# Two seven-product groups per pair in place of three in the out projection, and a table of paces for the weight sums kept in DRAM

## The chip, the cores and the metric

The kernel runs on one core of one Trainium2 chip. The metric is the device time of one execution in microseconds; before the change the median of 3 runs is 2548.02 us (2546.67 to 2549.71).

## The reference

A two-layer decoder trunk on 256 tokens of width 2048, all in float32. What matters here is the first layer and the chain of matrix products:

```python
zxbcdt = h @ in_proj                       # 2048 -> 2 x 4096 + 2 x 1024 + 64
z, xbc, dt_raw = split(zxbcdt)
...                                        # conv, SiLU, chunked scan -> y
y = y.reshape(bsz, seq, D_INNER) * silu(z)
yg = y.reshape(bsz, seq, SSM_GROUPS, 512)  # 8 groups of 512
yg = yg * rsqrt(mean(yg * yg, axis=-1) + EPS)
h = h + (yg.reshape(...) * gnorm_w) @ out_proj   # 4096 -> 2048
h = h + (silu(hn @ wg) * (hn @ wu)) @ w_down     # 2048 -> 2 x 5632 -> 2048
...                                        # second layer: attention (q, k, v, o), then the same kind of FFN
```

## The kernel before, in words

Every float32 product is made of three TensorE products in the type fp32r. A weight piece of two k-tiles by 512 columns (128x1024 in SBUF, `wraw`, 512 KB) is split by ScalarE into a rounded part `whi` (line 272) and by VectorE into the rest `wlo` (line 278); the activations lie in SBUF as such a pair already (`xT`, a "slot" of four k-tiles). Then hi*hi, hi*lo and lo*hi are added up in PSUM (lines 554 to 556). A piece makes 12 matmuls of 512 columns: two k-tiles, two halves of the tokens, three products.

`stream` runs over all pieces of the program in order. SyncE (SP) loads the weights, in units of 512 KB, six of them ahead (`RAW`); the splits are four pieces ahead of TensorE (`SPL`). A unit is loaded when the oldest of the six `wraw` buffers has been split, so the load queue follows VectorE.

Two neighbouring blocks of 512 output columns form a pair (`pair`). For some of the k groups (`kg`, four k-tiles each), named in `crossed`, the pair's 2x2x2 block product is made with seven products in place of eight (`Group`, `cross_step`, the order of the seven is f, d, c, a, e, g, b; lines 466 to 469). That takes 42 matmuls in place of 48, and needs sums of activation blocks (`xS`, made by `sums_from`, or from a finished slot by `add_sums`) and sums of weight blocks. Two of the weight sums of each group are made in DRAM: `next_sum` issues on SP a copy of one weight block into a DRAM tile `wsum` (line 375), and on GpSimd's queue the adding of the other block to the sum that was copied before (line 377). `sums` is one list over the whole program, in the order of use: the out projection, the first FFN's up and down projections, the attention's out projection, the second FFN's.

When a sum is made is set in `stream`: at every n-th unit loaded, `PACE` calls `next_sum` once. `PACE = (24, 224, 6, 10)` starts at unit 24, with n = 6 up to unit 224 and n = 10 from there. When a unit that is a sum comes up for loading and the sum is not made, `load` calls `next_sum` until it is: the next copy is issued, the adding is issued, and the load waits on SP until the adding has landed. All later loads stand behind it.

The out projection (8 groups kg, two pairs) crosses the groups `WOUT = (2, 4, 6)`. In a pair the uncrossed groups are laid out as left-block pieces (L) first and right-block pieces (R) behind them, with all the R put ahead of the next crossed group, so the first pair runs L0 L1 R0 R1 G2 L3 R3 G4 L5 R5 G6 L7 R7. Ahead of it stand the eight z blocks; block g gives `z_done(g)` (SiLU) and then `gate_y(g)`: multiply (line 1061), square (1064), the root on GpSimd (573), scale (1069), eight transposes on TensorE (586) and the split into the slot `ys[g]`. Gates run one after the other. The L pieces of the pair use PSUM buffers that z block 6 frees, the R pieces those of block 7, whose SiLU waits for gate 5. When the first group of a pair comes to its second product, d, `finish_all(False)` puts everything of the gates that is still open ahead of it, since the group takes four PSUM banks.

Of the kernel before, what the change touches and what calls it, by code (L numbers as in the profile page):

```python
# [24 lines left out]
G = 8  # L25
# [8 lines left out]
BIG = 1e30  # L34
KT = 4

WOUT, DN0, DN1 = (2, 4, 6), (3, 7), (3, 5, 7, 9)

WARM = 9
RAW = 6  # L40
SPL = 4

PACE = (24, 224, 6, 10)


LAT = 0.4
# [185 lines left out]
def kernel(ctx: ExitStack, tc: tile.TileContext, xT_d, x_d, cols_d, rows_d, wdt_d, win_d,  # L232
# [17 lines left out]
    def nm(s):  # L250
        uid[0] += 1
        return f"{s}_{uid[0]}"
# [4 lines left out]
    def bank(shape):  # L257
        return mis.tile(shape, F32, tag="mis", name=nm("mis"))
# [109 lines left out]
    def next_sum():  # L368


        new = next((v for v in sums if v.tile is None), None)
        old = next((v for v in sums if v.tile is not None and not v.made), None)
        if new is not None:
            new.tile = dram.tile([P, 2, NB], F32, name=nm("wsum"))
            nc.sync.dma_start(out=new.tile, in_=new.one)
        if old is not None:
            nc.gpsimd.dma_start(out=old.tile, in_=old.other, accum_op=ALU.add)  # L377
            old.made = True
# [8 lines left out]
    def load(u, apart=False, before=None):  # L387
        u.raw = wraw.tile([P, len(u.ks), u.width], F32, tag="wraw", name=nm("wraw"))
        src = u.src
        if isinstance(src, Sum):  # L390
            while not src.made:
                next_sum()
            src = src.tile
        for js in u.pieces if apart else [range(len(u.ks))]:
            if before is not None:
                before([u.ks[j] for j in js])
            nc.sync.dma_start(out=u.raw[:, js[0]:js[-1] + 1, :], in_=src[:, js[0]:js[-1] + 1, :])
# [24 lines left out]
    def split_cross(group, name):  # L422

        us = group.units

        def add(out, in0, in1):
            flow.work("V", 1.22, flow.at["E"])
            nc.vector.tensor_tensor(out=us[out].raw, in0=us[in0].raw, in1=us[in1].raw, op=ALU.add)  # L428

        place, dead = {"e": "c", "b": "c"}, {"f": "f", "c": "d", "a": "a", "g": "g", "b": "c"}  # L430
        late = {"c": ("c", "c", "d"), "e": ("c", "c", "g")}
        src = us[place.get(name, name)].raw
        hi = wspl.tile([P, 2, NB], F32R, tag="whi", name=nm("whi"))
        lo = wspl.tile([P, 2, NB], F32R, tag="wlo", name=nm("wlo"))
        split(hi, lo, src)
        ready = flow.work("V", 1.22, flow.work("A", 1.05, flow.at["E"]) + LAT)
        if name in late:
            add(*late[name])
        if name in dead:
            us[dead[name]].dead = True  # L440
        return hi, lo, ready
# [40 lines left out]
    def stream(pre_load, pre_split):  # L482
        pieces, units = [], []
        for b in blocks:
            for u in b.units if isinstance(b, Block) else b:
                if isinstance(u, Group):
                    pieces += [(u, n) for n in Cross.ORDER]
                    units += u.units.values()
                else:
                    pieces += [(u, ks) for ks in u.pieces]  # L490
                    units.append(u)
        parts = {}
        loaded, dead = [0], [0]

        def load_on():
            while dead[0] < len(units) and units[dead[0]].dead:
                dead[0] += 1
            while loaded[0] < min(dead[0] + RAW, len(units)):
                i = loaded[0]
                if i in pre_load:  # L500
                    pre_load[i]()
                pace = PACE[2] if i < PACE[1] else PACE[3]
                if i >= PACE[0] and i % pace == pace - 1:
                    next_sum()
                load(units[i], i == 0, load_x0 if i < 2 else None)
                loaded[0] += 1

        def split_to(n):
            for i in range(len(parts), min(n, len(pieces))):
                u, js = pieces[i]  # L510
                if i in pre_split:
                    pre_split[i]()
                parts[i] = split_cross(u, js) if isinstance(u, Group) else split_piece(u, js)
                load_on()

        load_on()
        split_to(SPL - 1)
        held = deque()
        for i, (u, ks) in enumerate(pieces):
            split_to(i + SPL)  # L520
            if isinstance(u, Group):
                cross_step(u, ks, parts[i])
                continue
            b = u.blk
            nk = KT * len(b.xs)
            hi, lo, ready = parts[i]
            flow.work("E", 0.0, ready)
            if u.width < NB:
                if b.ps is None:
                    b.ps = bank([2 * u.width, T])  # L530
                for j, k in enumerate(u.ks[n] for n in ks):
                    both = hi[:, j].rearrange("p a n -> p (a n)")
                    s = slot_of(b.xs[k // KT])
                    nc.tensor.matmul(b.ps, lhsT=both, rhs=s[:, 0, k % KT, :], start=k == 0, stop=False)
                    nc.tensor.matmul(b.ps, lhsT=both, rhs=s[:, 1, k % KT, :], start=False, stop=k == nk - 1)
                flow.work("E", 0.22 * len(ks))
                if ks is u.pieces[-1]:
                    b.task = spawn(b.done(b.ps))
                continue
            if b.ps is None:  # L540
                held.append(b)
                if len(held) > 2:
                    flow.finish(held.popleft().task, evac=True)
                b.ps = [acc.tile([P, u.width], F32, tag="acc", name=nm("acc")) for _ in range(NT)]
            last = b.after is None and u is b.units[-1] and ks is u.pieces[-1]
            order = [(j, t) for j in range(len(ks)) for t in range(NT)]
            if last:
                order = [(j, t) for t in range(NT) for j in range(len(ks))]
            for n, (j, t) in enumerate(order):
                k = u.kg * KT + u.ks[ks[j]]  # L550
                s = slot_of(b.xs[k // KT])
                xh = s[:, 0, k % KT, t * P:(t + 1) * P]
                xl = s[:, 1, k % KT, t * P:(t + 1) * P]
                nc.tensor.matmul(b.ps[t], lhsT=xh, rhs=hi[:, j, :], start=u is b.units[0] and ks[j] == 0, stop=False)  # L554
                nc.tensor.matmul(b.ps[t], lhsT=xh, rhs=lo[:, j, :], start=False, stop=False)  # L555
                nc.tensor.matmul(b.ps[t], lhsT=xl, rhs=hi[:, j, :], start=False,  # L556
                                 stop=last and j == len(ks) - 1)
                if n % 2 == 1:
                    flow.work("E", STEP)
                    flow.pump()  # L560
            if last:
                finish_block(b)
        flow.finish_all()
# [59 lines left out]
    def add_sums(dst, apart=True):  # L623


        def run():
            if not dst.task.done:
                yield dst.task
            s = dst.tile
            for half in range(2):  # L630
                if apart:
                    y, x = (lambda c: (c[:, 0], c[:, 1]))(phase.tile([P, 2, NB], F32, tag="c4", name=nm("ysum")))
                else:
                    y, x = tok("y"), None
                y = y.rearrange("p (f t) -> p f t", t=T)
                part = [s[:, i, 2 * half:2 * half + 2, :].bitcast(F32) for i in range(2)]
                nc.vector.tensor_tensor(out=y, in0=part[0], in1=part[1], op=ALU.add)
                yield V(0.66)
                yield from sums_from(dst, half, y, x)
        dst.adder = spawn(run(), flow.lazy)  # L640
# [396 lines left out]
    ys = [Slot() for _ in range(G)]  # L1037

    def z_done(g):
        def run(ps):  # L1040
            if g >= 2:
                yield ys[g - 2].task
            zs = []
            for t in range(NT):
                z = tok("zs")
                nc.scalar.activation(z, ps[t], AF.Silu, scale=rstd[:, t:t + 1])  # L1046
                zs.append(z)
                yield A(0.57, SILU)
            ys[g].task = spawn(gate_y(g, zs), flow.mid)
            if g >= G - 2:  # L1050
                for kg in WOUT:
                    if (kg < G - 2) == (g == G - 2):
                        add_sums(ys[kg])
        return run

    def gate_y(g, zs):
# [325 lines left out]
```

## Time and profile before

| | |
|---|---|
| median of 3 runs | 2548.02 us (2546.67 to 2549.71) |
| the profiled execution | 2547.09 us; its span 2545.3 us, 1.8 us lie around the span |
| TensorE busy | 2497.1 us, 98%; granted clock 0.989 in the mean |
| VectorE, ScalarE, GpSimd busy | 1990.1, 1443.6 and 137.0 us |
| moved by DMA | 638.56 MB; 120 sums are copied and added |

A busy TensorE is not all of it: the granted clock has two levels, 1.2 and 2.4 GHz, and a clock of 0.5 of full speed stands for the lower one. So time is lost where TensorE is idle, and where it works at the lower level. The stages in order of time: z and scan up to about 521 us, out projection, first FFN up and down, attention from about 1400, second FFN up from about 1820, down from about 2300 to the end.

### The profile page before, as it was taken

The page shows a single profiled execution, that of the slowest core. Times are in us where ns is not written, and L with a number is a line of the kernel's source. Part 1 is how long each engine was busy: PE and PEld are TensorE (multiplying, and loading weights), DVE is VectorE, ACT ScalarE, POOL GpSimd, SP SyncE. Part 2 cuts the span into 40 slices and gives each one's busy share as a digit, 9 for nine tenths or more (in the row PEclk, how much of TensorE's full clock was granted, in tenths as well). Part 3 has the DMA queues.
Part 4 walks back from the last instruction along what each step waited for, and adds up shares of the span by engine and source line. Part 5 has one row for each costly group of instructions (what it writes and reads, how often), then busy time and mean ns, then how long its engine had stood idle before and what let it go on. Part 6 is the DMA issues. An engine that isn't in the chain of part 4 may idle for free.

```text
span 2545.3 us, 31879 instructions
## 1 busy us (share of the span) xinstructions
PE 2497.1 (98%) x11410; PEld 2064.3 (81%) x11410; DVE 1990.1 (78%) x2577; ACT 1443.6 (57%) x1815; POOL 137.0 (5%) x172
## 2 busy tenths in 40 slices
PE   9999999979999999999999999999999999999899
PEld 7888888868888888888888888888888877787787
DVE  6777777768788999998756667778889987788667
ACT  6566565555555665655544555566656654554444
POOL 0000000000000000000000011000000000000000
PEclk9999999989999999999999999999999999999899
DMA  7887777749988888887778777766778899987886
GB/s 265 252 254 240 224 234 240 237 144 307 278 256 252 290 259 282 258 290 238 256 228 268 221 210 226 205 193 219 237 260 280 270 296 270 293 293 233 264 281 230
DMA packets 174606, 638.56 MB, mean 251 GB/s; under 512 B 19408, under 2 KB 20064, under 8 KB 172912
## 3 DMA queue, kind: packets, MB, share of 16 engines
q1 hardware_dynamic: 155664, 563.05, 63.7%
q0 software_dynamic: 18784, 73.49, 15.8%
q8 instruction: 89, 1.46, 0.2%
q14 instruction: 69, 0.57, 0.1%
HBM read 634.28 MB, written 128.01 MB: 299 GB/s over the span
## 4 chain that ended last, share of the span: by engine, by line
PE 68%; DMA 6%; DVE 3%; ACT 1%; issue 1%; SPq 0%; POOL 0%; ACTq 0%; POOLq 0%; DVEq 0%
PE acc L554 16%; PE acc L556 16%; PE acc L555 16%; PE mis L467 4%; PE mis L469 4%; PE mis L466 3%; DMA wsum<-in_gu_dram 3%; PE acc L467 3%; PE acc L469 3%; PE acc L466 3%; DMA wraw<-wsum 2%; DVE wlo L278 2%; PE mis L586 1%; DMA wsum<-in_dn_dram 1%; ACT whi L272 1%
## 5 line engine op out<-in xcount | busy, mean ns | idle before, releaser
L278 DVE TENSOR_TENSOR wlo<-wraw,whi 128x1024 fp32r<-128x1024 f32 (+1 forms) x965 | 1155.2, 1221 | 344.6 <-ACT whi L272 337.4
L272 ACT CAST whi<-wraw 128x1024 fp32r<-128x1024 f32 (+1 forms) x968 | 994.8, 1050 | 713.9 <-PE acc L556 436.1
L554 PE MATMUL acc<-whi,xT 128*128 128x512 f32 x2464 | 970.6, 394 | 5.5 <-ACT zs L1046 5.1
L555 PE MATMUL acc<-wlo,xT 128*128 128x512 f32 x2464 | 961.3, 390 | 0.8 <-DVE wlo L278 0.8
L556 PE MATMUL acc<-whi,xT 128*128 128x512 f32 x2464 | 961.6, 390 | 0.0
L554 PEld LDWEIGHTS acc<-whi,xT 128*128 128x128 f32 x2464 | 463.9, 188 | 102.0 <-ACT zs L1046 5.3
L556 PEld LDWEIGHTS acc<-whi,xT 128*128 128x128 f32 x2464 | 463.5, 188 | 97.8
L555 PEld LDWEIGHTS acc<-wlo,xT 128*128 128x128 f32 x2464 | 464.0, 188 | 95.8 <-DVE wlo L278 1.8
L280 DVE SCALAR_TENSOR_TENSOR wlo<-wraw,cols,whi 128x512 fp32r<-128x512 f32 x192 | 134.6, 748 | 70.7 <-ACT whi L274 70.3
L274 ACT ACTIVATE whi<-wraw,cols 128x512 fp32r<-128x512 f32 x192 | 127.6, 718 | 72.1 <-PE acc L556 55.0
L466 PE MATMUL mis<-whi,xS 128*128 128x512 f32 x360 | 146.0, 406 | 20.1 <-ACT whi L272 20.1
L467 PE MATMUL mis<-wlo,xS 128*128 128x512 f32 x360 | 146.4, 407 | 3.9 <-DVE wlo L278 3.9
L428 DVE TENSOR_TENSOR wraw<-wraw,wraw 128x1024 f32<-128x1024 f32 x120 | 147.0, 1225 | 4.1
L469 PE MATMUL mis<-whi,xS 128*128 128x512 f32 x360 | 145.3, 404 | 0.0
L377 POOL DMA_DIRECT2D wsum<-in_gu_dram x80 | 66.2, 828 | 1105.4 <-DMA wsum<-in_gu_dram 1105.4
L466 PEld LDWEIGHTS mis<-whi,xS 128*128 128x128 f32 x360 | 70.5, 196 | 37.5 <-ACT whi L272 22.7
L467 PE MATMUL acc<-wlo,xT 128*128 128x512 f32 x232 | 91.6, 395 | 2.5 <-DVE wlo L278 2.4
L466 PE MATMUL acc<-whi,xT 128*128 128x512 f32 x232 | 91.1, 393 | 0.0
L469 PE MATMUL acc<-whi,xT 128*128 128x512 f32 x232 | 90.6, 390 | 0.0
L467 PEld LDWEIGHTS mis<-wlo,xS 128*128 128x128 f32 x360 | 70.5, 196 | 22.2 <-DVE wlo L278 7.3
L469 PEld LDWEIGHTS mis<-whi,xS 128*128 128x128 f32 x360 | 70.7, 196 | 14.7
L272 ACT CAST xT<-mis 128x512 fp32r<-128x512 f32 x52 | 28.0, 589 | 54.4 <-PE mis L586 54.4
(250 smaller groups left out, 2138.9 us busy)
## 6 DMA issues: line engine op xcount, KB each, us to landing
wraw<-in_gu_dram SPq DMA_DIRECT2D x312, 512.0 KB, 6.3
wraw<-in_dn_dram SPq DMA_DIRECT2D x164, 512.0 KB, 6.0
wraw<-in_win_dram SPq DMA_DIRECT2D x159, 512.0 KB, 5.9
wraw<-wsum SPq DMA_DIRECT2D x120, 512.0 KB, 5.8
wsum<-in_gu_dram SPq DMA_DIRECT2D x80, 512.0 KB, 6.6
wsum<-in_gu_dram POOLq DMA_DIRECT2D x80, 512.0 KB, 8.3
wraw<-in_wout_dram SPq DMA_DIRECT2D x58, 512.0 KB, 6.8
wraw<-in_wq_dram SPq DMA_DIRECT2D x32, 512.0 KB, 4.8
```

What stands on the lines that cost most here:

```text
L272: nc.scalar.copy(out=hi, in_=src)
L274: nc.scalar.activation(hi, src, AF.Copy, scale=scal)
L278: nc.vector.tensor_tensor(out=lo, in0=src, in1=hi.bitcast(F32), op=ALU.subtract)
L280: nc.vector.scalar_tensor_tensor(out=lo, in0=src, scalar=scal, in1=hi.bitcast(F32), op0=ALU.mult, op1=ALU.subtract)
L377: nc.gpsimd.dma_start(out=old.tile, in_=old.other, accum_op=ALU.add)
L428: nc.vector.tensor_tensor(out=us[out].raw, in0=us[in0].raw, in1=us[in1].raw, op=ALU.add)
L466: nc.tensor.matmul(ps, lhsT=xh, rhs=hi[:, p, :], start=group.first and p == 0 and name not in own, stop=False)
L467: nc.tensor.matmul(ps, lhsT=xh, rhs=lo[:, p, :], start=False, stop=False)
L469: nc.tensor.matmul(ps, lhsT=xl, rhs=hi[:, p, :], start=False, stop=stop and p == 1)
L554: nc.tensor.matmul(b.ps[t], lhsT=xh, rhs=hi[:, j, :], start=u is b.units[0] and ks[j] == 0, stop=False)
L555: nc.tensor.matmul(b.ps[t], lhsT=xh, rhs=lo[:, j, :], start=False, stop=False)
L556: nc.tensor.matmul(b.ps[t], lhsT=xl, rhs=hi[:, j, :], start=False, stop=last and j == len(ks) - 1)
```

## The change

Three things: the out projection crosses the groups 4 and 6, and no longer 2; the activation sums of both slots are started at the last gate, where those of slots 2 and 4 were started at the last but one; and the pace is a table by unit: none up to 24, 6 up to 224, 9 up to 440, 7 up to 760, and 9 from there.

```diff
-WOUT, DN0, DN1 = (2, 4, 6), (3, 7), (3, 5, 7, 9)
+WOUT, DN0, DN1 = (4, 6), (3, 7), (3, 5, 7, 9)
-PACE = (24, 224, 6, 10)
+PACE = ((24, 0), (224, 6), (440, 9), (760, 7), (2000, 9))
...
-                pace = PACE[2] if i < PACE[1] else PACE[3]
-                if i >= PACE[0] and i % pace == pace - 1:
+                pace = next(n for end, n in PACE if i < end)
+                if pace and i % pace == pace - 1:
                     next_sum()
...
             ys[g].task = spawn(gate_y(g, zs), flow.mid)
-            if g >= G - 2:
+            if g == G - 1:
                 for kg in WOUT:
-                    if (kg < G - 2) == (g == G - 2):
-                        add_sums(ys[kg])
+                    add_sums(ys[kg])
```

The units are counted over the program: the out projection holds units 161 to 230 before (161 to 228 now, a crossed group has five units and an uncrossed one four), the second FFN's up projection 650 to 845 (648 to 843 now), its down projection up to 941 (939). There are 120 sums before and 116 now. The pairs of the out projection are now laid out L0 L1 L2 L3 R0 R1 R2 R3 G4 L5 R5 G6 L7 R7.

SP's queue in the second FFN's up projection, before; `in_gu_dram` is the weights, L375 the copy of a new sum, `wraw<-wsum` the load of a sum:

```order
L375 DMA wsum_17735<-in_gu_dram 128x1024
L397 DMA wraw_17734<-wsum_17686 128x1024
L397 DMA wraw_17757<-in_gu_dram 128x1024
...
L375 DMA wsum_17907<-in_gu_dram 128x1024
L397 DMA wraw_17906<-wsum_17735 128x1024
L375 DMA wsum_17911<-in_gu_dram 128x1024
L397 DMA wraw_17914<-wsum_17907 128x1024
L397 DMA wraw_17927<-in_gu_dram 128x1024
```

SP's queue at the same place now (the load of the same weights' sums):

```order
L397 DMA wraw_17722<-wsum_14968 128x1024
L397 DMA wraw_17736<-wsum_15118 128x1024
L397 DMA wraw_17756<-in_gu_dram 128x1024
L375 DMA wsum_17776<-in_dn_dram 128x1024
...
L397 DMA wraw_17908<-wsum_15243 128x1024
L397 DMA wraw_17910<-wsum_15501 128x1024
L397 DMA wraw_17923<-in_gu_dram 128x1024
```

Before, sum 17907 is copied one sum ahead of its own load. Now the sums loaded here were copied some 130 units earlier, and the copies that stand here are for the down projection. Over the whole program the least distance from a sum's copy to its load is 1 unit before and 62 units now; before, the distances under 10 units all lie from unit 749 on.

TensorE's order at the first crossed group of the out projection's first pair, before (`mis<-ident,xs` are the transposes of the gates 6 and 7; f goes to `acc`, d to `mis`):

```order
L469 MATMUL acc_4601<-whi_4615,xS_4406 128x512
L466 MATMUL acc_4601<-whi_4615,xS_4406 128x512
L467 MATMUL acc_4601<-wlo_4616,xS_4406 128x512
L469 MATMUL acc_4601<-whi_4615,xS_4406 128x512
L586 MATMUL mis_4698<-ident,xs_2529 128x128 x4
L586 MATMUL mis_4707<-ident,xs_2529 128x128 x4
L586 MATMUL mis_4728<-ident,xs_2529 128x128 x4
L586 MATMUL mis_4737<-ident,xs_2529 128x128 x4
L466 MATMUL mis_4746<-whi_4633,xT_3521 128x512
```

The same place now:

```order
L469 MATMUL acc_4704<-whi_4831,xS_4585 128x512
L466 MATMUL acc_4704<-whi_4831,xS_4585 128x512
L467 MATMUL acc_4704<-wlo_4832,xS_4585 128x512
L469 MATMUL acc_4704<-whi_4831,xS_4585 128x512
L466 MATMUL mis_4901<-whi_4851,xT_3971 128x512
L467 MATMUL mis_4901<-wlo_4852,xT_3971 128x512
```

And where the gate 6's transposes stand now, between L2 and L3:

```order
L555 MATMUL acc_4479<-wlo_4534,xT_3521 128x512
L556 MATMUL acc_4479<-whi_4533,xT_3521 128x512
L586 MATMUL mis_4629<-ident,xs_2529 128x128 x4
L586 MATMUL mis_4638<-ident,xs_2529 128x128 x4
L554 MATMUL acc_4478<-whi_4562,xT_3742 128x512
```

The transposes of gate 5 moved from behind 48 matmuls of the pair (L0, L1) to behind the first 12; those of gate 6 stand behind 72 of them in place of 102, those of gate 7 behind 132 in place of 102, inside R1; nothing of the gates stands in the first group any more, which now begins behind 192 matmuls in place of 96.

## Rows read from the trace of the kernel before

**Rows 1.** The page's parts 1 and 3: busy time and share; the DMA queues.

```profile
PE 2497.1 (98%) x11410; PEld 2064.3 (81%) x11410; DVE 1990.1 (78%) x2577; ACT 1443.6 (57%) x1815; POOL 137.0 (5%) x172
...
q1 hardware_dynamic: 155664, 563.05, 63.7%
q0 software_dynamic: 18784, 73.49, 15.8%
```

**Rows 2.** Stretches: us, busy (count) by engine, clock, DMA share, GB/s.

```profile
520.00:580.00 60.00, 46.07 (x192) 36.98 (x192) 39.95 (x65) 33.70 (x54) 4.61 (x6) 0.86 0.52 160
600.00:700.00 100.00, 100.00 (x449) 82.49 (x448) 80.78 (x88) 59.29 (x74) 5.68 (x7) 1.00 0.94 294
1420.00:1740.00 320.00, 320.00 (x1552) 267.99 (x1551) 225.84 (x461) 187.29 (x344) 30.98 (x31) 1.00 0.70 209
1860.00:2060.00 200.00, 199.79 (x898) 165.27 (x897) 182.66 (x183) 122.19 (x132) 8.18 (x10) 1.00 0.86 276
2080.00:2200.00 120.00, 104.74 (x432) 83.18 (x431) 87.39 (x86) 57.45 (x63) 8.17 (x10) 0.93 0.92 268
2200.00:2260.00 60.00, 60.00 (x273) 49.79 (x272) 53.98 (x57) 34.11 (x37) 3.27 (x4) 1.00 0.99 326
2340.00:2420.00 80.00, 70.18 (x266) 55.41 (x265) 56.06 (x63) 36.26 (x38) 5.70 (x7) 0.87 0.89 264
```

**Rows 3.** Who waited for whom: us in total, times, longest.

```profile
PE mis L466 <- ACT whi L272: 20.1, 6, 4.8
...
SPq L397 <- DMA wsum<-in_gu_dram: 61.8, 7, 11.5
SPq L397 <- DMA wsum<-in_dn_dram: 35.5, 3, 13.0
```

**Rows 4.** One sum in order of time: start us, us, what [idle before].

```profile
2122.27 0.50 SPq L375 DMA_DIRECT2D wsum<-in_gu_dram  x1
...
2128.86 0.81 POOL L377 DMA_DIRECT2D wsum<-in_gu_dram  x1 [16.54 <-DMA wsum<-in_gu_dram]
...
2135.95 0.33 SPq L397 DMA_DIRECT2D wraw<-wsum  x1
...
2141.43 2.94 ACT L272 CAST whi<-wraw 128x1024 fp32r<-128x1024 f32 x3 [9.36 <-DMA wraw<-wsum]
...
2142.52 0.80 PE L466 MATMUL mis<-whi,xS 128*128 128x512 f32 x1 [4.75 <-ACT whi L272]
```

**Rows 5.** Gate SiLU of line 749 in each FFN's up projection, durations, first and last start.

```profile
L749 ACT ACTIVATE d<-d,rs x11: 716/721/731, 755.3 to 1173.1; 128x512 f32<-128x512 f32 x11
...
L749 ACT ACTIVATE d<-d,rs x11: 716/720/729, 1847.4 to 2289.4; 128x512 f32<-128x512 f32 x11
```

**Rows 6.** TensorE in order of time, first pair of the out projection.

```profile
520.95 0.39 PE L554 MATMUL acc<-whi,xT 128*128 128x512 f32 x1
...
531.60 0.39 PE L556 MATMUL acc<-whi,xT 128*128 128x512 f32 x1
531.83 1.03 PE L586 MATMUL mis<-ident,xs 128*128 128x128 f32 x8
537.93 0.80 PE L554 MATMUL acc<-whi,xT 128*128 128x512 f32 x1 [5.06 <-ACT zs L1046]
...
555.50 0.33 PE L586 MATMUL mis<-ident,xs 128*128 128x128 f32 x1 [2.56 <-ACT xs L1069]
...
563.05 2.37 PE L586 MATMUL mis<-ident,xs 128*128 128x128 f32 x8 [5.89 <-ACT xs L1069]
...
574.41 0.39 PE L554 MATMUL acc<-whi,xT 128*128 128x512 f32 x1
```

**Rows 7.** ScalarE and VectorE there, in order of time.

```profile
516.05 0.62 ACT L272 CAST xS<-ysum 128x512 fp32r<-128x512 f32 x1 [6.96 <-DVE ysum L618]
...
519.93 1.29 DVE L1061 TENSOR_TENSOR xs<-xs,zs 128x512 f32<-128x512 f32 x2
...
526.00 1.34 ACT L1069 ACTIVATE xs<-xs,rs 128x512 f32<-128x512 f32 x2 [1.03 <-POOL rs L573]
```

## The prediction

> **What bounds the kernel now.** I read the page first: TensorE is busy 98% of the span, VectorE 78%, the DMA engines 80% [rows 1]. So TensorE sets the time, and what can be won is where it is idle or runs at the lower clock: 2545.3 - 2497.1 = 48.2 us idle, and a mean clock of 0.989, that is 0.011 x 2545 = 28 us. Then the stretches of the span, to see where this lies: 520 to 580 (busy 46.07 of 60, clock 0.86), 2080 to 2200 (104.74 of 120, 0.93) and 2340 to 2420 (70.18 of 80, 0.87); the stretches beside them are full at clock 1.00 [rows 2]. Then the list of waits: in 20.1 us of its idle time TensorE waits, six times, for the split of a weight in a crossed group, and SP itself stands 61.8 + 35.5 = 97.3 us in ten waits for a `wsum` [rows 3]. Last, the order of time inside the three stretches [rows 4, 6, 7].
>
> The two late stretches have one cause, to be read in one sum: SP issues its copy at 2122.27, GpSimd the adding at 2128.86, when the copy has landed; SP, which holds all later loads meanwhile, loads the sum at 2135.95; ScalarE gets it at 2141.43 after 9.36 us of idling, TensorE at 2142.52 [rows 4]. That is 20 us from copy to use, in which SP stands for 9.7 us in the mean of its ten waits [rows 3], and six `wraw` buffers do not cover it.
>
> The first stretch is the chain of the last gates. TensorE waits 5.06 us at 537.93 for the SiLU of z block 7 (its PSUM buffers are wanted by R0, and the SiLU waits for gate 5), 2.56 us at 555.50 and 5.89 us at 563.05 for the scaled rows of gates 6 and 7, whose transposes stand in front of product d [rows 6].
>
> **The change, part by part.**
>
> *Late sums.* Now every sum is made 62 units or more ahead of its load, so the wait on SP goes, and with it what follows on ScalarE and TensorE. What it costs now I take in two ways. The two FFN up stages do the same work; from the first to the last gate SiLU, ten block pairs, the first takes 1173.1 - 755.3 = 417.8 us and the second 2289.4 - 1847.4 = 442.0 [rows 5]: 24.2 us. By idle time and clock the stretch 2080 to 2200 gives 15.3 + 0.07 x 120 = 23.7 [rows 2], so that way of counting holds, and I use it for the down projection, which has no twin: 9.8 + 0.13 x 80 = 20.2 us [rows 2]. Together -44.4 us, about 6.3 for each of seven stalls. Bounds: 0, if the sums made earlier only move the delay, and -46, if the small idle of the neighbouring stretches goes too.
>
> *The first pair of the out projection.* From 520.95 (start of L0) to 574.41 (the first matmul behind the first crossed group) are 53.5 us. In them lie 96 + 42 matmuls and 24 transposes. The pitch of a matmul at the full clock is (531.60 - 520.95) / 47 = 0.2266 us, eight transposes take 1.03 [rows 6]: 31.3 + 3.1 = 34.4 us. So 19.1 us are lost here (by idle and clock of 520 to 580: 13.9 + 8.4 = 22.3 [rows 2], where idle at the low clock counts twice).
>
> What is late next, in the new order? ScalarE no longer stands 6.96 us in front of the first `xS`, and on VectorE the multiplies of gate 5, which began 3.9 us behind the sums that this `xS` waited for (519.93 against 516.05), have one split of weights in front of them where those sums and two splits stood [rows 7]. From the multiplies to the scaled rows the gate took 519.93 to 526.00 + 1.34, with two splits of weights and half of a slot's sums in between [rows 7]; begun near 516 it is done by 521 to 523, and its transposes stand behind 12 matmuls, at 520.95 + 2.7 = 523.7. Gate 6 begins behind the split of gate 5's slot, at about 527, and has 8 us until its transposes at 520.95 + 72 x 0.2266 + 1.0 = 538.3. Gate 7 begins at about 541.7 and its transposes come another 60 matmuls and eight transposes later, at 552.9: 11 us for a chain of 7 to 8. R0 wants the PSUM of z block 7 at 520.95 + 96 x 0.2266 + 2.1 = 544.8; the SiLU stands in ScalarE's order ahead of gate 6's second square, at about 532. The sums of slots 4 and 6 run on VectorE between these, and the first crossed group wants them at about 567.6. Every margin is 1 us or more, so I take -19.1 whole. Bounds: 0, if each wait finds a new place, and -22.3.
>
> *Three groups to two.* Two pairs, one group each, 48 matmuls in place of 42: 12 x 0.2266 = +2.7 us, on TensorE, which sets the time. The sums of slot 2 and the adds inside the two groups leave VectorE, and four sums leave the queues; none of that is waited for outside the stretch already counted, so 0.
>
> *The sums that now run earlier.* They fall beside loads: pace 9 for 10 in the first FFN, 7 in its down projection, in the attention and for the first 110 units of the second up projection. I cost it at 0, since DMA time is to be had, and this cover has to be checked. A sum is two transfers of 0.524 MB; by queue, 0.637 x 2545 / 563.05 = 2.88 us of all engines per MB on SP's and 0.158 x 2545 / 73.49 = 5.47 on GpSimd's [rows 1], so 4.4 us for each sum. The stretch 1860 to 2060 has ten sums in 200 us and a share of 0.86 [rows 2]. At pace 7 and the same progress, 18 units in 41.8 us, there would be 12.3: 0.86 + 2.3 x 4.4 / 200 = 0.91. The out projection ran 100 us at a share of 0.94 with seven sums, and 2200 to 2260 ran at 0.99, both with TensorE busy throughout and the clock at 1.00 [rows 2]. The attention has room from 0.70. Bounds: 0 (nothing is won by it) and +24, the price of the four stalls of one up stage, if loads come late as often as they do now.
>
> The Trainium skill, DMA: Bandwidth & Descriptors, "Where 436 GB/s comes from", speaks against this part: it puts the HBM side at about 358 GB/s for each core, with both cores of a pair streaming. An estimate by that page: 276 GB/s moved, and the written side of copy and adding on top, would come to some 350 GB/s at pace 7, so the loads would be at the edge and the added sums could cost time. The same count over 600 to 700 gives 294 + 7 x 1.05 MB / 100 us = 367 GB/s with TensorE busy 100.00 of 100 us [rows 2], so here the trace does not bear the limit out, and the sum above stays as it is.
>
> **The sum.** 2547.1 - 44.4 - 19.1 + 2.7 = 2486.3 us against the profiled execution's own time; the median of the runs stands 0.9 us above that execution, so 2487.2. Two of the margins are thin, and I forecast 2488 us.
>
> **The rivals.**
> 1. The waits of the first pair find new places: the transposes of gate 5 stand 36 matmuls earlier than before, and if its chain does not start earlier TensorE stands 3 to 5 us there, falls to the low clock, and gates 6 and 7 follow late. For it: the gates run one after the other, and the margins are short. Against it: the work that held ScalarE and VectorE there is gone. Price up to the whole 19.1: 2507.
> 2. The DMA engines are too full in the second up projection: `wraw` loads land late, and half of the seven late stalls come back in other places. For it: shares of 0.9 and more. Against it: 0.94 and 0.99 were run without a wait. Price 22: 2510.
> 3. The late stalls are not the chain's but due to crossed groups under full queues, and remain: 2487 + 44 = 2531, or 2533 at most. Against it: the first up projection has the same groups and no stall.
> 4. The other side: the sums at pace 7 and 9 make the loads of every crossed group late, 20 groups in the second up projection and eight in the down projection, at the 6.3 us that one stall costs now: 28 x 6.3 = 176 us, 2660. It decides from ten stalls on, since 60.8 / 6.3 = 9.7; fewer only eat into the gain. Against it: 0.91 is under what already ran full.
>
> **How the numbers follow.** Forecast 0.78, with a range of its own from 2482 to 2496 (the bounds of the two stall terms below, some 8 us of thin margins above); rival 1 0.09, rival 2 0.08, rival 3 0.02, rival 4 0.03. The range of 8 in 10 goes from 2481 to 2506: it takes in the forecast and the milder half of rivals 1 and 2, and leaves out some 0.14. Below 0.2% a measurement of this kernel can't tell a change from none, that is 5 us; only rival 4 is not faster, and of its 0.03 next to nothing falls within 5 us. Faster 0.96, same 0.01, slower 0.03.
>
> **What would show it.** Right: no wait of SP for a `wsum`; the second up projection takes 418 us between its first and last gate SiLU; TensorE's clock is 1.00 from 600 us to the end; between 520 and 580 no idle time of 2 us or more, and 12 matmuls more in the out projection. Wrong: ScalarE waiting for `wraw` by several us in the second up projection at a share near 1 (rival 2); TensorE waiting for the scaled rows or the SiLU inside L0 to R1 (rival 1); stalls at 2080 to 2420 with every sum long landed (rival 3).

## The result, and the profile after

The changed kernel takes 2488.99 us in the median of 4 runs (2487.53 to 2490.49), the kernel before 2548.64 beside it; the ratio is 0.9767, with a 95% interval from 0.975 to 0.9784. That is 59.7 us less, for a forecast of 60.

The page of the changed kernel, parts 1 and 3 (busy us, share, instructions; the DMA queues), against [rows 1]:

```profile
PE 2475.1 (100%) x11422; PEld 2053.5 (83%) x11422; DVE 1972.9 (79%) x2555; ACT 1435.4 (58%) x1807; POOL 133.9 (5%) x168
...
q1 hardware_dynamic: 154800, 559.90, 64.3%
q0 software_dynamic: 18208, 71.39, 15.6%
```

Its stretches (us, busy time and count of each engine, clock, DMA share, GB/s), against [rows 2]:

```profile
520.00:580.00 60.00, 60.00 (x279) 49.94 (x278) 48.74 (x70) 39.62 (x57) 5.45 (x7) 1.00 0.74 223
1860.00:2060.00 200.00, 200.00 (x904) 166.03 (x903) 183.25 (x185) 120.85 (x131) 9.80 (x12) 1.00 0.90 292
2000.00:2200.00 200.00, 200.00 (x905) 166.03 (x904) 182.10 (x182) 119.03 (x128) 8.96 (x11) 1.00 0.88 282
2280.00:2360.00 80.00, 78.95 (x346) 64.36 (x345) 70.38 (x82) 46.87 (x49) 1.66 (x2) 1.00 0.74 243
2360.00:2460.00 100.00, 100.00 (x443) 82.66 (x442) 71.07 (x65) 49.04 (x48) 0.00 (x0) 1.00 0.70 237
```

The first two lossy stretches of before are full and at clock 1.00. The work of the third, 2340 to 2420, now runs some 40 us earlier, and in 2280 to 2360 TensorE is idle for 1.05 us, also at clock 1.00. A wait of SP for a `wsum` no longer occurs. TensorE's waits that are left (us in total, times, longest; the three longest groups) are a few of half a microsecond to 1.6, against the 20.1 us in six waits of [rows 3]:

```profile
PE acc L554 <- ACT whi L272: 2.2, 2, 1.6
PE acc L467 <- DVE wlo L278: 1.8, 3, 0.6
PE mis L1298 <- POOL ident masks.py:199: 1.4, 1, 1.4
```

The gate SiLU in the two FFN up stages, against [rows 5]:

```profile
L749 ACT ACTIVATE d<-d,rs x11: 714/716/727, 739.5 to 1157.8; 128x512 f32<-128x512 f32 x11
...
L749 ACT ACTIVATE d<-d,rs x11: 714/719/728, 1832.1 to 2249.1; 128x512 f32<-128x512 f32 x11
```

TensorE in order of time at the last gates, against [rows 6]: the eight transposes of gates 5, 6 and 7 now run in the middle of the pair's matmuls with no idle time in front of them.

```profile
522.45 0.39 PE L554 MATMUL acc<-whi,xT 128*128 128x512 f32 x1
...
525.17 1.03 PE L586 MATMUL mis<-ident,xs 128*128 128x128 f32 x8
525.96 0.48 PE L554 MATMUL acc<-whi,xT 128*128 128x512 f32 x1
...
539.67 1.03 PE L586 MATMUL mis<-ident,xs 128*128 128x128 f32 x8
...
554.16 1.03 PE L586 MATMUL mis<-ident,xs 128*128 128x128 f32 x8
```

From these times and those of [rows 5, 6] the span divides as follows:

| stretch | before | after | difference |
|---|---|---|---|
| start to L0 of the out projection | 520.95 | 522.45 | +1.5 |
| L0 to the first FFN's first gate SiLU | 234.4 | 217.1 | -17.3 |
| first FFN up, first to last SiLU | 417.8 | 418.3 | +0.5 |
| from there to the second FFN's first SiLU | 674.3 | 674.3 | 0.0 |
| second FFN up, first to last SiLU | 442.0 | 417.0 | -25.0 |
| from there to the end | 255.9 | 238.0 | -17.9 |
| span | 2545.3 | 2487.1 | -58.2 |

### The profile page after: what moved, and what is told of

It reads as the page before. It is cut to its first block, busy times and chain, and to the rows that moved or that the text cites. A ratio compares the mean times of both kernels' runs of the same rounds, so it can differ in the third digit from the quotient of the medians.

```text
span 2487.1 us, 31833 instructions
## 1 busy us (share of the span) xinstructions
PE 2475.1 (100%) x11422; PEld 2053.5 (83%) x11422; DVE 1972.9 (79%) x2555; ACT 1435.4 (58%) x1807; POOL 133.9 (5%) x168
## 4 chain that ended last, share of the span: by engine, by line
PE 97%; DVE 1%; DMA 1%; ACT 0%; issue 0%; SPq 0%; ACTq 0%; DVEq 0%
PE acc L554 23%; PE acc L556 23%; PE acc L555 23%; PE mis L469 4%; PE mis L466 4%; PE mis L467 4%; PE acc L467 3%; PE acc L469 3%; PE acc L466 3%; PE mis L586 1%; PE mis L1023 1%; DVE wlo L278 1%; PE mis L893 0%; DVE wraw L428 0%; DMA wraw<-in_dn_dram 0%; PE mis L1029 0%
## 5 line engine op out<-in xcount | busy, mean ns | idle before, releaser
L554 PEld LDWEIGHTS acc<-whi,xT 128*128 128x128 f32 x2496 | 469.2, 188 | 99.8 <-ACT whi L272 2.9
L556 PEld LDWEIGHTS acc<-whi,xT 128*128 128x128 f32 x2496 | 468.8, 188 | 98.4
L555 PEld LDWEIGHTS acc<-wlo,xT 128*128 128x128 f32 x2496 | 469.4, 188 | 97.4 <-DVE wlo L278 2.4
L467 PE MATMUL mis<-wlo,xS 128*128 128x512 f32 x348 | 135.5, 389 | 0.4 <-DVE wlo L278 0.4
L469 PE MATMUL mis<-whi,xS 128*128 128x512 f32 x348 | 135.4, 389 | 0.0
L466 PE MATMUL mis<-whi,xS 128*128 128x512 f32 x348 | 135.4, 389 | 0.0
L467 PEld LDWEIGHTS mis<-wlo,xS 128*128 128x128 f32 x348 | 65.3, 188 | 14.6 <-DVE wlo L278 0.9
L466 PEld LDWEIGHTS mis<-whi,xS 128*128 128x128 f32 x348 | 65.3, 188 | 13.6
L469 PEld LDWEIGHTS mis<-whi,xS 128*128 128x128 f32 x348 | 65.3, 188 | 13.5
```

Source lines behind the costliest of these rows:

```text
L466: nc.tensor.matmul(ps, lhsT=xh, rhs=hi[:, p, :], start=group.first and p == 0 and name not in own, stop=False)
L467: nc.tensor.matmul(ps, lhsT=xh, rhs=lo[:, p, :], start=False, stop=False)
L469: nc.tensor.matmul(ps, lhsT=xl, rhs=hi[:, p, :], start=False, stop=stop and p == 1)
```

## The experiments

**The pace table alone.** The kernel before with the new table; the out projection as it was.

```diff
-PACE = (24, 224, 6, 10)
+PACE = ((24, 0), (224, 6), (440, 9), (760, 7), (2000, 9))
```

> The kernel before with the new pace table alone: three groups 2, 4, 6 in the out projection, their activation sums started as before, 120 sums, the least distance from a sum's copy to its load 28 units. Theory (two separate gains: the late sums give 43, the first pair 17): 2548.6 - 43 = 2505 us; SP waits for no wsum, the stretch 520 to 580 looks as before (46 of 60 us busy), the second FFN's up projection takes 417 us between its first and last gate SiLU. Rival (the late stalls are due to full queues, not to the chain): over 2530.

Measured: 2509.88 us, ratio 0.9831 (0.9818 to 0.9845). The late stalls are gone, the first pair's are not. A stretch of it, its waits of TensorE, and its second FFN's SiLU:

```profile
520.00:580.00 60.00, 46.01 (x191) 37.09 (x190) 40.02 (x64) 32.06 (x53) 4.29 (x5) 0.86 0.51 148
```

```profile
PE mis L586 <- ACT xs L1069: 8.8, 3, 6.0
PE acc L554 <- ACT zs L1046: 5.1, 1, 5.1
```

```profile
L749 ACT ACTIVATE d<-d,rs x11: 716/720/725, 1853.0 to 2272.1; 128x512 f32<-128x512 f32 x11
```

The two gains lie in different places, as in the theory; 5 us less were won than expected: the second up stage took 419.1 us where 417 were said, and the first, where no loss was expected, 421.3 in place of the 417.8 of before (TensorE was idle for 1.2 us between 900 and 940). So the new table costs some 3.5 us in the first up stage when the list holds 120 sums; with 116, in the changed kernel, that stage takes 418.3.

**The out projection alone.** The changed kernel with the old pace.

```diff
-PACE = ((24, 0), (224, 6), (440, 9), (760, 7), (2000, 9))
+PACE = ((24, 0), (224, 6), (2000, 10))
```

> The changed kernel with the old pace (6 up to unit 224, 10 from there): 116 sums. Four sums fewer at ten units each put the whole list 40 units ahead, so only one sum is loaded within 3 units of its copy, where before it were eight. Theory A (the pace table is what cures the late stalls): 2548.6 - 17 = 2531 us. Theory B (a stall comes only where the distance is 3 units or less, so that the four sums that are left out cure most of them by themselves): 2489 plus one to three stalls of 6.3 us, 2495 to 2508, with three waits of SP for a wsum at most that reach TensorE.

Measured: 2495.06 us, ratio 0.9777 (0.9763 to 0.979). Theory B. TensorE's only wait of its kind, and SP's waits for a `wsum`, against [rows 3]:

```profile
PE mis L466 <- ACT whi L272: 3.4, 1, 3.4
```

```profile
SPq L397 <- DMA wsum<-in_gu_dram: 18.3, 4, 7.8
SPq L397 <- DMA wsum<-in_dn_dram: 6.7, 4, 4.7
```

One stall is left, between 2100 and 2120, where the one sum with a distance of 1 unit stands; the 18 sums with a distance of 4 to 9 units, behind which SP waits too (25 us in eight waits in all), give none. It costs 6 us against the changed kernel (the second up stage takes 423.3 us in place of 417.0), the price of one stall. So most of the late gain does not need the table: four sums fewer put the list 40 units ahead, and 55.6 us (2550.7 - 2495.1) less the 17.3 of the out projection leave 38 for the late stages; by the stages of the profiled execution it is 37.

**A head start, and nothing else.** The kernel before with a quicker first pace.

```diff
-PACE = (24, 224, 6, 10)
+PACE = (24, 224, 5, 10)
```

> The kernel before with pace 5 in place of 6 up to unit 224, all else as before: seven sums more are made in the first stage, so the list is some 70 units ahead from there; the pace of 10 in the later stages is kept. No sum of the second up projection is then loaded within 3 units of its copy; three of the down projection still are, one unit behind it. Theory (a stall is a sum whose copy stands 3 units or less ahead of its load): the 24 us of the up projection go, the 20 us of the down projection stay, 2550 - 24 = 2526 us, 417 us between the first and last gate SiLU of the second up projection. Rival (the pace inside the late stages is what decides): 2550.

Measured: 2525.48 us, ratio 0.9903 (0.9887 to 0.992), the number of the theory. The second up stage's SiLU, and SP's waits:

```profile
L749 ACT ACTIVATE d<-d,rs x11: 716/716/729, 1852.0 to 2269.6; 128x512 f32<-128x512 f32 x11
```

```profile
SPq L397 <- DMA wsum<-in_dn_dram: 35.0, 3, 12.5
```

The up stage takes 417.6 us, and the three waits that stay are those of the down projection, at the sums whose copy stands one unit ahead. The stall follows the distance from copy to load, not the stage and not the pace that is in force there. It is not a stall every time, though: of the six sums that the kernel before loads one unit behind their copy, one (SP loads it at 2165) left TensorE waiting for no more than half a microsecond.

**Where the sums start.** The changed kernel, with the sums of slot 4 started at the last gate but one.

```diff
-            if g == G - 1:
+            if g >= G - 2:
                 for kg in WOUT:
-                    add_sums(ys[kg])
+                    if (kg < G - 2) == (g == G - 2):
+                        add_sums(ys[kg])
```

> The changed kernel with the sums of slot 4 started at the last gate but one, as before, those of slot 6 at the last. Theory (the cover of 192 matmuls in front of the first group is what removes the waits; where the sums start is worth little): 2489, within 3 us. Rival (the sums on VectorE and ScalarE in front of gate 5 are what delays the gates): TensorE waits again 3 to 5 us inside L0 or R0 and its clock falls, 2493 to 2500.

Measured: 2488.58 us, ratio 0.9752 (0.9739 to 0.9766): no difference from the changed kernel. Its first stretch has 0.7 us of idle time:

```profile
520.00:580.00 60.00, 59.33 (x274) 48.89 (x274) 46.55 (x66) 39.73 (x60) 6.19 (x7) 1.00 0.76 233
```

**Three groups with their sums behind the last gate.**

```diff
-WOUT, DN0, DN1 = (4, 6), (3, 7), (3, 5, 7, 9)
+WOUT, DN0, DN1 = (2, 4, 6), (3, 7), (3, 5, 7, 9)
```

> The changed kernel with the groups 2, 4, 6 crossed and all three slots' sums started at the last gate. Theory (the cover decides): the first group again begins behind 96 matmuls, the transposes of the last gates stand in front of its product d, so most of the 19 us comes back: 2489 - 3 + 14 to 22 = 2500 to 2508. Rival (the place of the sums decides): 2486, the 12 matmuls less.

Measured: 2506.3 us, ratio 0.9817 (0.9804 to 0.9831): the theory again, with one part that it did not have. Of the 18.9 us by which its profiled span is longer than the changed kernel's, 13.7 come before the first gate SiLU (753.2 against 739.5) and 5.2 in the first up stage, which takes 423.5 us; the list holds 120 sums again, as with the table alone:

```profile
L749 ACT ACTIVATE d<-d,rs x11: 715/717/725, 753.2 to 1176.7; 128x512 f32<-128x512 f32 x11
```

The first two waits of TensorE are for the sums of slot 2, which now come too late for product f, and for the scaled rows of a gate:

```profile
PE acc L466 <- ACT xS L272: 5.4, 1, 5.4
PE mis L586 <- ACT xs L1068: 5.3, 1, 5.3
```

Of the change in the out projection it is the 192 matmuls ahead of the first crossed group that pay; the place of the sums pays nothing with them, and does not cure the waits without them (2506.3 us here and 2509.88 with the table alone, with intervals that overlap).

**More load on the DMA engines, first way.** Every copy twice.

```diff
             nc.sync.dma_start(out=new.tile, in_=new.one)
+            spare = dram.tile([P, 2, NB], F32, name=nm("spare"))
+            nc.sync.dma_start(out=spare, in_=new.one)
```

> The changed kernel with every copy of a weight block into a DRAM sum made twice, the second into a tile that nothing reads: 116 transfers of 0.524 MB more, 1.5 us of all DMA engines each. Theory (the DMA engines have room at this pace): DMA share up by 0.03 to 0.04 in the up projections, time the same, 2489 within 4 us. Rival (the queues are at their edge): loads land late at crossed groups, TensorE stalls return, 2500 or more.

Measured: 2495.45 us, ratio 0.9786 (0.9771 to 0.98). Between the two: some 6 us over the changed kernel by the medians, 5 by the ratios, whose intervals overlap. The spare copy also stands in SP's queue ahead of the next loads, so the run does not part fuller engines from a longer queue. The stretches of both up stages, and ScalarE's waits for loads (10.0 and 3.6 us in the changed kernel for the same two):

```profile
760.00:1140.00 380.00, 378.14 (x1693) 310.41 (x1692) 338.33 (x339) 222.18 (x240) 14.65 (x18) 1.00 0.89 301
1860.00:2060.00 200.00, 199.26 (x898) 164.52 (x897) 180.61 (x182) 117.24 (x128) 10.60 (x13) 1.00 0.97 325
```

```profile
ACT whi L272 <- DMA wraw<-in_gu_dram: 33.7, 25, 3.9
ACT whi L272 <- DMA wraw<-wsum: 22.7, 11, 3.8
```

**Second way: pace 6 to the end.**

```diff
-PACE = ((24, 0), (224, 6), (440, 9), (760, 7), (2000, 9))
+PACE = ((24, 0), (2000, 6))
```

> The changed kernel with pace 6 from unit 24 to the end of the list: the sums are 105 units or more ahead, all made by unit 720, and the first up projection runs with 18 / 6 = 3 sums for each block pair in place of 2. Theory (DMA room is enough: the out projection ran at this pace with no wait): share about 0.94 in the first up projection, 2489 within 4 us. Rival (a smaller n than 9 costs there): TensorE waits for late loads in the first up projection, more than 418 us between its first and last gate SiLU, 2495 to 2515.

Measured: 2495.19 us, ratio 0.9787 (0.9772 to 0.9802). The first up stage took 1160.0 - 738.1 = 421.9 us, 3.6 more than in the changed kernel, and the second 419.9, at shares of

```profile
760.00:1140.00 380.00, 379.09 (x1698) 311.47 (x1698) 338.98 (x339) 222.38 (x242) 22.01 (x27) 1.00 0.94 300
1860.00:2060.00 200.00, 197.92 (x891) 163.41 (x890) 179.99 (x181) 117.82 (x128) 5.72 (x7) 1.00 0.81 264
```

The run before took 423.2 and 418.8 us for the two. So the room was there, but it ends soon: 2 to 5 us are lost in each up stage, in waits of under 1 us each. The mean share does not order these losses (2.9 us at 0.81, 4.9 at 0.89, 3.6 at 0.94, 1.8 at 0.97), so it is not what decides; it may be which transfers fall beside each other, but that was not tried. No stall with a fall of the clock comes of it in the up stages: rival 4's price, 6.3 us for each group, is not reached in either run.

**Another table, for what is left.** 5 up to unit 224, 10 up to 440, 7 up to 760, 10 from there.

> The changed kernel with another table: 5 up to unit 224, 10 up to 440, 7 up to 760, 10 from there, so that seven sums more are made in the first stage, where the DMA engines have most room, and the up projections go back to a pace of 10. Theory (what the changed kernel still loses to late loads is small, 14 us of ScalarE's waits of which TensorE sees next to nothing): 2489, within 2 us. Rival (the up projections at 9 and 7 cost some time): 2484 to 2486.

Measured: 2488.72 us, ratio 0.9759 (0.9743 to 0.9774). This table wins nothing more.

**Three groups further back.** The groups 3, 4 and 6; and 4, 5 and 6 with the table of the last run.

```diff
-WOUT, DN0, DN1 = (4, 6), (3, 7), (3, 5, 7, 9)
+WOUT, DN0, DN1 = (3, 4, 6), (3, 7), (3, 5, 7, 9)
```

> The changed kernel with the out projection's groups 3, 4 and 6 crossed: three groups as before, but the first one stands behind 144 matmuls, 32.6 us, in place of 96 before and 192 now. Theory (the cover decides, and the last gate's transposes were ready by some 30 us behind L0): 12 matmuls less and no new wait, 2489 - 2.7 = 2486 us. Rival (32.6 us is too short): TensorE waits in the first group for gate 7, 2490 to 2496.

> The kernel e11 with the out projection's groups 4, 5 and 6 crossed: 12 matmuls less, the first group behind 192 matmuls, but three groups in a row, in which VectorE has 11 us of work for 9.5 us of TensorE each. Theory (VectorE limits neighbouring groups, as the run with 3, 4, 6 showed in waits of 0.4 to 0.7 us for wlo): two neighbouring groups more cost more than the 2.7 us, 2492 to 2500. Rival (the loss with 3, 4, 6 was the late sums of slots 3 and 4 only): 2486.

Measured: 2497.62 us, ratio 0.9794 (0.978 to 0.9809), and 2511.15 us, ratio 0.9848 (0.9829 to 0.9866). Both lose, and not by the gates. With 3, 4, 6, where the list holds 120 sums, 3.7 of the 10.9 us by which the profiled span is longer than the changed kernel's lie in the first up stage (422.0 us). In the out projection the waits of TensorE are for `wlo` and for sums; in order of time, the two neighbouring groups:

```profile
561.84 0.50 PE L467 MATMUL mis<-wlo,xS 128*128 128x512 f32 x1 [0.65 <-DVE wlo L278]
...
564.24 0.50 PE L467 MATMUL mis<-wlo,xS 128*128 128x512 f32 x1 [0.74 <-DVE wlo L278]
...
567.91 0.50 PE L467 MATMUL acc<-wlo,xT 128*128 128x512 f32 x1 [0.62 <-DVE wlo L278]
...
573.64 0.50 PE L466 MATMUL acc<-whi,xS 128*128 128x512 f32 x1 [1.98 <-ACT xS L272]
```

With 4, 5, 6 the worst wait stands behind each pair's groups, where the next left block wants PSUM that VectorE has not emptied yet:

```profile
PE acc L554 <- DVE h L674: 11.1, 2, 5.9
```

I had priced neighbouring groups at 3 to 11 us and the second run lost 22, most of it in these two waits and in the fall of the clock behind them (0.83 between 700 and 720). But they do not show what neighbouring groups cost, since the groups do not stand "in a row": where the last two crossed groups are neighbours, `pair` puts the last one behind the left pieces that remain (`adjacent`), so the order is G4 G5 L7 G6 R7. VectorE then needs no more time than in the changed kernel to add the group's parts and the left block to `h`, 12.2 us there (598.30 to 610.5) and 12.5 here (607.99 to 620.5; the last of the three adds from `acc` is the right block's):

```profile
598.30 0.68 DVE L674 TENSOR_TENSOR h<-h,d 128x512 f32<-128x512 f32 x1
...
609.22 1.27 DVE L674 TENSOR_TENSOR h<-h,acc 128x512 f32<-128x512 f32 x2
```

```profile
607.99 0.68 DVE L674 TENSOR_TENSOR h<-h,d 128x512 f32<-128x512 f32 x1
...
619.20 1.87 DVE L674 TENSOR_TENSOR h<-h,acc 128x512 f32<-128x512 f32 x3
620.02 0.77 PE L554 MATMUL acc<-whi,xT 128*128 128x512 f32 x1 [5.85 <-DVE h L674]
```

First the changed kernel, then this one. In the former L7 and R7, 48 matmuls or 10.9 us, stand behind the last group and cover this; here only R7 does, 24 matmuls or 5.4 us, and the rest is the wait. The groups 4, 5 and 6 in the order G4 G5 G6 were not tried. No version tried is faster than the changed kernel beyond the noise.

## Why the prediction was right, point by point

*Late sums, -44.4 forecast.* Measured -25.0 in the up stage (24.2 said) and -17.9 from there to the end (20.2 said), -42.9 together. The size of the up stage came from its twin and was good to 1 us; the down projection's, from idle time and clock, was 2.3 too large, partly because idle time at the low clock counts twice in it (0.8 us, an estimate: 1.6 us of waits lie there), partly because 1.05 us of new waits for `wlo` stand at its first crossed groups (78.95 of 80 us). The number of stalls was wrong: the prediction says seven, four of them in the up stage, but [rows 3] has six such waits of TensorE, and the trace three in each stage. So a stall cost 42.9 / 6 = 7.1 us and not 6.3; that moves the price of rival 4, but not the sum, which was not built from the number of stalls. The cause, the chain from copy to load, is shown by the head start and by the out projection alone: the stalls go and stay with the distance. What I did not see is that the table is not needed for most of it. I counted the distances now, and gave the gain to the change as a whole; the 116 sums in place of 120 do 37 to 38 of the 43 us under the old pace, and the table alone some 41. They are two cures for one thing, so the parts do not add up (40.8 + 55.6 is far over 59.7).

*The first pair, -19.1, and 12 matmuls, +2.7.* Together -16.4 forecast, -17.3 measured from L0 to the first SiLU. The margins held: the gates' transposes ran at 525.2, 539.7 and 554.2, where 523.7, 538.3 and 552.9 were said, each 1.3 to 1.5 later because L0 itself began 1.5 later. The scaled rows of gate 6 were ready at 534.80 + 1.34 = 536.1:

```profile
534.80 1.34 ACT L1068 ACTIVATE xs<-xs,rs 128x512 f32<-128x512 f32 x2 [0.51 <-POOL rs L573]
```

That is 1 us later than worked out, with 3.5 us in hand. (The prediction's "8 us until its transposes" is a slip: from 527 to 538.3 are 11.3 us, and 8 is what the gate's chain takes, 528.26 to 536.14 here.) That the cover does it and not the place of the sums is shown by the two runs that part them.

*The sums beside the loads, 0.* Right at this pace: 0.90 of DMA share in 1860 to 2060 (0.91 was worked out), TensorE busy 200.00 of 200 us. The two runs with more load show the edge that I had set too far off: I took 0.94 and 0.99 of [rows 2] as proof of room, and the up stages lose 2 to 5 us each at mean shares of 0.81 to 0.97. A stage's mean share was the wrong measure of the cover; what decides within a stage stays open. The changed kernel itself is near this edge: its table costs 3.5 to 5 us in the first up stage in the three runs that use it with 120 sums.

The Trainium skill, DMA: Bandwidth & Descriptors, "Where 436 GB/s comes from", puts the HBM side at some 358 GB/s for each of two cores. By the count used for the forecast (an estimate: what was moved, and the written side of the transfers from DRAM to DRAM on top) the changed kernel is at 292 + 12 x 1.05 MB / 200 us = 355 GB/s in 1860 to 2060 with no wait, and the run with every copy twice at 325 + 13 x 1.57 MB / 200 us = 427, with 0.7 us of idle time in 200. With this one core running, the trace goes past that figure.

*What lay outside.* The start up to L0 took 1.5 us more in the profiled execution, with TensorE idle for 4.6 of the first 20 us in place of 2.6; the program is the same there. So the closeness of the total is in part luck: against the sum of 2486.3 for the profiled execution, 2488.84 were measured, made up of +1.5 at the start, +1.5 in the late sums, +0.5 in the first up stage and -0.9 in the first pair.

*The rivals.* 1 fell: no idle time between 520 and 580. 2 fell at this pace. 3 fell with the head start: the same groups under the same pace of 10, and no stall in the up stage. 4 fell, and its price for a group is not met even under heavier load in the up stages.

## What to carry to other kernels

Where work is prepared ahead of its use at a fixed pace, look at the least distance between preparing and using over the whole program, not at the mean pace: a lag of a few items that grows slowly stays invisible until it reaches the point where the in-order queue has to wait for its own transfer, and then items cost stalls. A little head start, or a few items fewer, anywhere earlier can cure most of it without a new pace (here four sums fewer left one stall of six, a head start of seven sums left three), so test the parts of such a change one by one before giving the gain to one of them. And a chain of short operations in front of a barrier can be hidden by moving the barrier behind more of the main engine's own work.

## What was not expected of the hardware

Six stalls of TensorE, of 2.6 to 4.8 us each, cost 42.9 us in the late stages, 7.1 each: smaller waits came behind them, and the granted clock fell to its lower level after each (0.87 over 2340 to 2420 [rows 2]). Waits of under 1 us in the up stages under full DMA queues left it at 1.00, with pace 6 even two of 0.80 and 0.71 us close to each other; two of 0.88 and 0.76 us, in the run with 4, 5, 6, did not (0.91 between 580 and 600). GpSimd's DMA queue, 62.9 of whose 73.5 MB are the adding, took 5.47 us of all engines per MB and SP's, nearly all plain, 2.88 [rows 1], so by these figures a sum made of one copy and one adding costs about as much as three plain loads.
